# Two half tiles of their own buffers for the high and low parts of every weight tile

## The chip, the cores and the metric

The kernel runs on one core of one Trainium2 chip. The metric is the device time of one execution in microseconds (us). The core has five engines that each work through their own queue of instructions in order: TensorE (PE in the rows; its weight loads have a row of their own, PEld), VectorE (DVE), ScalarE (ACT), GpSimd (POOL) and SyncE (SP), whose queue issues nearly all transfers here. They wait for each other through semaphores.

## The reference, cut to what matters

Two layers over 1024 latent tokens and 256 context tokens, all in float32. Nearly all the work is products with weights:

```python
for layer in range(2):
    u  = modulate(rmsnorm(x,  n1), sh1,  sc1)  @ w_in      # x: 1024 x 1024, w_in: 1024 x 3088
    uc = modulate(rmsnorm(xc, n1), csh1, csc1) @ w_in      # xc: 256 x 1024
    y  = concat(mlstm(u, uc), neighbourhood_attention(u, uc), rglru(u, uc)) @ w_out
    x  = x + g1 * y
    h  = modulate(rmsnorm(x, n2), sh2, sc2)
    x  = x + g2 * (square(relu(h @ w1)) @ w2)              # w1: 1024 x 4096, w2: 4096 x 1024
```

The same is done for the context, except for its output side in the last layer. The twelve modulation vectors of a layer are products of a conditioning vector with `w_mod` (1024 x 6144). The mixers hold small products, scans and a softmax; they are not touched here.

## The kernel before

**Weights.** A weight tile is 128 partitions by 1024 float32 numbers (in two places by 1088): 8 K tiles of 128 columns (`w_fm`, line 204, for products with 128 output columns), or 4 K tiles of 256 or 272 columns. `load_w` (line 185) loads it with one transfer (two for half of the output projection) into `wr`, which has two buffers, and splits it into two float32r parts: ScalarE copies the high part into `wh` (line 200), VectorE subtracts it from the raw tile into the low part `wl` (line 201). `wh` and `wl` have two buffers each. There are 340 such tiles. With `early` (the first of the two tiles of a token-major projection, 16 tiles in all) the split is done in two steps of half the columns into the same buffer. A buffer is free again when the last product that reads any of it is done.

**Products.** The activations are kept as high and low parts too, and each product is three products: high by high, low by high, high by low. `proj_fm` (line 427, products on line 436) makes a 128-column tile of a projection for blocks of 256 or 512 tokens, 24 products for each block, over the K tiles in order. `proj_tm` (line 441, products on line 451) goes over the ten tiles of 128 tokens with two weight tiles, K tiles 0 to 3 in the first and 4 to 7 in the second. `oproj` (products on line 1325) is the output projection in halves of four K tiles.

**The order of the stages**, twice: the LRU's and the mLSTM's input projections beside their scans; the attention's input projections in two groups (`na_group`), the first beside the mLSTM's chunks; the attention with half of the output projection between its steps (from 510 us in layer 0, from 2100 us in layer 1); the other half; then the MLP. `mlp_group` takes 512 hidden columns at a time: four tiles of the first weight (line 436) and four of the second, each of four K tiles (line 1477), whose products VectorE adds to the residual (line 1481). The MLP runs its eight groups first for one part of the tokens and then for the other: in layer 0 for context and first half (256 + 512 columns), then for the second half (512); in layer 1 for 512 and 512. So 24 of its 32 group runs have products of 512 columns only.

**Modulation steps** run beside all this. In layer 0's mLSTM output and attention projections, 32 steps each load 512 KB of `w_mod` into `mr`, one buffer, and TensorE multiplies it (line 274). In layer 0's first MLP part, 48 steps for layer 1 are done by VectorE, 16 or 8 operations each (lines 310 and 312), and every second or fourth step TensorE transposes the sums (`mod_sum`, line 323): 16 sums in all.

**The order of instructions** is not the order of the text. A scheduler sorts each engine's queue when the program is built, by its own model of when operands are ready, so that another shape or another buffer moves instructions on every engine.

## Time and profile before

| | us |
|---|---|
| three executions | 3126.22, 3126.86, 3132.38 |
| their median | 3126.86 |
| span of the profiled execution, first to last instruction | 3122.6 |
| median less that span | 4.3 |
| TensorE busy in the span | 3016.5 |

The profile is of one execution, and durations below are its own. The span leaves out what lies before the first and after the last instruction; the 4.3 us are taken for that. Busy time of TensorE counts each product from its start to its modelled end, and ends overlap the next start, so a small gap between two products need not show as idle time: the distance of two starts tells it.

### The profile page before, as it was taken

To read this page: it belongs to the slowest core of one execution; us is meant where nothing else is said; L and a number is where in the kernel's file an instruction comes from. 1 tells how busy PE (TensorE), PEld (TensorE's weight loads), DVE (VectorE), ACT (ScalarE), POOL (GpSimd) and SP (SyncE) were. 2 spreads that over 40 slices of the span, in tenths; PEclk is the share of its full clock that TensorE was granted. 3 is DMA by queue.
4 is the path that set the end of the run, shared out by engine and by line. 5 is a ranking of instruction groups with operands and counts; after the bars stand their busy time and mean duration, and the time that the engine had idled before them with its cause. 6 is when DMAs were issued, how large, how long until landed. Compare 5 with 4: busy or idle time off the path is not lost.

```text
span 3122.6 us, 47473 instructions
## 1 busy us (share of the span) xinstructions
PE 3016.5 (97%) x18250; PEld 2553.0 (82%) x18250; DVE 1898.7 (61%) x4318; ACT 1129.1 (36%) x2011; POOL 288.9 (9%) x252
## 2 busy tenths in 40 slices
PE   7999998999899999999999999998899999999999
PEld 6888887878788888887778889997787777887877
DVE  5757654887887666455444584755787444444444
ACT  4632223674422222233222453234564223332222
POOL 0410010122200000010000511002222000000000
PEclk9999999999899999999999999999999999999999
DMA  9624667865233444233333532348753332343333
GB/s 272 223 73 124 174 172 206 234 186 176 67 109 109 123 127 124 79 108 99 92 94 95 176 122 82 101 123 222 223 169 113 95 95 88 99 117 90 93 96 93
DMA packets 531098, 410.73 MB, mean 132 GB/s; under 512 B 27580, under 2 KB 496536, under 8 KB 530872
## 3 DMA queue, kind: packets, MB, share of 16 engines
q1 hardware_dynamic: 519448, 387.41, 42.1%
q0 software_dynamic: 8576, 15.00, 1.5%
q10 hardware_dynamic: 2848, 5.28, 0.6%
q8 instruction: 144, 2.36, 0.3%
q14 instruction: 82, 0.67, 0.1%
HBM read 339.72 MB, written 67.53 MB: 130 GB/s over the span
## 4 chain that ended last, share of the span: by engine, by line
PE 70%; DVE 11%; DMA 10%; issue 2%; ACT 2%; SPq 1%; POOL 0%; ACTq 0%; DVEq 0%; POOLq 0%
PE psa L436 15%; PE psa L1477 14%; PE psq L436 5%; PE psp L436 5%; PE psp L1477 5%; PE psq L1477 5%; PE psp L451 4%; DMA mr<-in_w_mod_dram 4%; PE psq L451 4%; PE psp L1325 2%; DVE ma L312 2%; PE psc L718 2%; DVE wl L201 1%; PE psa L1325 1%; PE psb L688 1%
## 5 line engine op out<-in xcount | busy, mean ns | idle before, releaser
L200 ACT ACTIVATE wh<-wr 128x1024 fp32r<-128x1024 f32 (+3 forms) x356 | 361.6, 1021 | 946.5 <-PE psa L1477 307.3
L201 DVE TENSOR_TENSOR wl<-wr,wh 128x1024 fp32r<-128x1024 f32 (+3 forms) x356 | 425.0, 1198 | 386.4 <-ACT wh L200 380.0
L436 PE MATMUL psa<-xlo,wh 128*128 128x512 f32 (+1 forms) x856 | 319.7, 374 | 2.2 <-DVE xlo L412 2.2
L436 PE MATMUL psa<-xh,wh 128*128 128x512 f32 (+1 forms) x856 | 319.4, 373 | 2.4 <-ACT xh L411 2.3
L436 PE MATMUL psa<-xh,wl 128*128 128x512 f32 (+1 forms) x856 | 319.6, 373 | 1.4 <-DVE wl L201 1.4
L1477 PE MATMUL psa<-hl,wh 128*128 128x512 f32 (+1 forms) x768 | 286.0, 373 | 0.6 <-DVE hl L211 0.6
L1477 PE MATMUL psa<-hh,wh 128*128 128x512 f32 (+1 forms) x768 | 284.2, 375 | 0.3 <-ACT wh L200 0.3
L1477 PE MATMUL psa<-hh,wl 128*128 128x512 f32 (+1 forms) x768 | 277.9, 373 | 0.6 <-DVE wl L201 0.6
L1481 DVE SCALAR_TENSOR_TENSOR res<-psa,modt,res 128x512 f32<-128x512 f32 (+1 forms) x192 | 131.0, 693 | 170.3 <-PE psa L1477 169.9
L436 PEld LDWEIGHTS psa<-xh,wh 128*128 128x128 f32 x856 | 162.1, 190 | 33.4 <-ACT xh L411 3.1
L436 PEld LDWEIGHTS psa<-xlo,wh 128*128 128x128 f32 x856 | 162.1, 189 | 33.1 <-DVE xlo L412 2.6
L436 PEld LDWEIGHTS psa<-xh,wl 128*128 128x128 f32 x856 | 162.1, 189 | 32.3 <-DVE wl L201 2.2
L377 POOL TENSOR_TENSOR acc<-acc,nsq 128x512 f32<-128x512 f32 (+1 forms) x56 | 77.9, 1401 | 1026.9 <-ACT nsq L376 976.5
L1477 PEld LDWEIGHTS psa<-hh,wh 128*128 128x128 f32 x768 | 144.3, 188 | 34.6 <-ACT wh L200 8.6
L451 PE MATMUL psp<-wl,xh 128*128 128x256 f32 (+1 forms) x560 | 164.0, 293 | 4.3 <-DVE wl L201 4.2
L1477 PEld LDWEIGHTS psa<-hh,wl 128*128 128x128 f32 x768 | 144.3, 188 | 28.7 <-DVE wl L201 1.5
L1477 PEld LDWEIGHTS psa<-hl,wh 128*128 128x128 f32 x768 | 144.4, 188 | 27.4 <-DVE hl L211 0.8
L210 ACT ACTIVATE hh<-rl 128x512 fp32r<-128x512 f32 (+1 forms) x160 | 93.5, 589 | 202.1 <-DVE rl L1453 202.0
L451 PE MATMUL psp<-wh,xh 128*128 128x256 f32 (+1 forms) x560 | 161.9, 289 | 2.4 <-ACT wh L200 2.4
L451 PE MATMUL psq<-wh,xh 128*128 128x256 f32 (+1 forms) x560 | 161.7, 289 | 1.4 <-ACT usq L605 0.9
L451 PE MATMUL psq<-wl,xh 128*128 128x256 f32 (+1 forms) x560 | 160.6, 287 | 0.0
L451 PE MATMUL psp<-wh,xlo 128*128 128x256 f32 (+1 forms) x560 | 159.9, 286 | 0.0
(409 smaller groups left out, 7328.5 us busy)
## 6 DMA issues: line engine op xcount, KB each, us to landing
wr<-in_w_mlp_dram SPq DMA_DIRECT2D x256, 512.0 KB
mr<-in_w_mod_dram SPq DMA_DIRECT2D x92, 512.0 KB
wr<-in_w_in_dram SPq DMA_DIRECT2D x48, 512.0 KB
tab<-T_d SPq DMA_DIRECT2D x48, 384.0 KB
T_d<-E_d POOLq DMA_DIRECT2D x48, 256.0 KB, 6.6
ab<-row_d SPq DMA_DIRECT2D x36, 256.0 KB
xT_d<-res SPq DMA_DIRECT2D x4, 2048.0 KB
wr<-in_w_out_dram SPq DMA_DIRECT2D x32, 256.0 KB
```

The source lines that it names most:

```text
L200: act.activation(hi[:, a:b], raw[:, a:b], AF.Copy)
L201: dve.tensor_sub(lo[:, a:b], raw[:, a:b], hi[:, a:b].bitcast(F32))
L210: act.activation(hi, src32, AF.Copy)
L312: dve.scalar_tensor_tensor(a, raw[:, k], s[:, k], a, op0=OP.mult, op1=OP.add)
L377: pool.tensor_add(acc[bi], acc[bi], sq[:, :n])
L436: m = pe.matmul(t[:, :n], w[a][:, k, :], X[bi][b][:, k, :], start=(i == 0), stop=(i == 23))
L451: pe.matmul(t[:, :cols], X[bi][b][:, half * 4 + k, o:o + P], ws[half][a][:, k, :], start=(i == 0), stop=(i == 23))
L688: pe.transpose(t[:w, j * P:(j + 1) * P], S[e][:, o:o + w], permT)
L718: pe.matmul(to[64 * e:64 * e + 64, :P], vals[i][:w, 64 * e:64 * e + 64], PT[:w, e, i], start=(i == 0), stop=(i == nt - 1))
L1325: pe.matmul(t[:, :n], w[a][:, k, cc * P:(cc + 1) * P], Y[bi][b][:, k], start=(i == 0), stop=(i == 11))
L1477: m = pe.matmul(t[:, :n], w[a][:, k, cc * P:(cc + 1) * P], H[bi, k][b], start=(i == 0), stop=(i == 3 * GH - 1))
L1481: dve.scalar_tensor_tensor(xr[bi][:, ct], t[:, :n], G2[:, ct, v:v + 1], xr[bi][:, ct], op0=OP.mult, op1=OP.add)
```

## The change

Each half of the columns of a weight tile's high and low part becomes a tile of its own, with its own buffer: `wh` and `wl` have four buffers of 544 columns in place of two of 1088, the same space. Every tile is now split in two steps, first half first, the 16 `early` ones as well, so that ScalarE and VectorE have 680 splits each where they had 356, 324 more. A class `Halves` picks the half by the K tile, so products read what they read before. A half's buffer is free when the last product that reads that half is done. `wr` and its transfers are the same. The rest of the diff takes comments away.

```diff
-    def load_w(src, shape, early=False):
+    WHALF = WSZ // 2
+
+    class Halves:
+        def __init__(self, views, per):
+            self.views, self.per = views, per
+
+        def __getitem__(self, at):
+            p_, k, c_ = at
+            return self.views[k // self.per][p_, k % self.per, c_]
+
+    def load_w(src, shape):
         raw = wp.tile([P, WSZ], F32, name=nm("wr"), tag="wr", bufs=2)
-        hi = wp.tile([P, WSZ], F32R, name=nm("wh"), tag="wh", bufs=2)
-        lo = wp.tile([P, WSZ], F32R, name=nm("wl"), tag="wl", bufs=2)
...
-        cuts = [0, n // 2, n] if early else [0, n]
-        for a, b in zip(cuts, cuts[1:]):
-            act.activation(hi[:, a:b], raw[:, a:b], AF.Copy)
-            dve.tensor_sub(lo[:, a:b], raw[:, a:b], hi[:, a:b].bitcast(F32))
-        return (hi[:, :n].rearrange("p (k c) -> p k c", k=shape[0]),
-                lo[:, :n].rearrange("p (k c) -> p k c", k=shape[0]))
+        per = shape[0] // 2
+        h = n // 2
+        his, los = [], []
+        for i in range(2):
+            hi = wp.tile([P, WHALF], F32R, name=nm("wh"), tag="wh", bufs=4)
+            lo = wp.tile([P, WHALF], F32R, name=nm("wl"), tag="wl", bufs=4)
+            act.activation(hi[:, :h], raw[:, i * h:(i + 1) * h], AF.Copy)
+            dve.tensor_sub(lo[:, :h], raw[:, i * h:(i + 1) * h], hi[:, :h].bitcast(F32))
+            his.append(hi[:, :h].rearrange("p (k c) -> p k c", k=per))
+            los.append(lo[:, :h].rearrange("p (k c) -> p k c", k=per))
+        return Halves(his, per), Halves(los, per)
...
-                         .rearrange("(k p) c -> p k c", p=P), (4, 256), h_ == 0) for h_ in range(2)]
+                         .rearrange("(k p) c -> p k c", p=P), (4, 256)) for h_ in range(2)]
```

TensorE, SyncE and GpSimd have the same instructions as before. Some 2500 of TensorE's 16,800 stand elsewhere in its queue, and 233 of SyncE's 1284. Line numbers after the change are 15 higher (10 higher for the weights' transfer, 14 for the splits). Three places follow; numbers behind names count tiles and differ between the two programs.

**TensorE, at the third weight tile of the second product in an MLP group of layer 0's second part.** `wh_15960` and `wl_15961` are the parts of that tile, `wh_15994` of the fourth; `psa`, `psp`, `psq` are accumulators, one for each block of output columns. Before:

```order
L1477 MATMUL psa_15945<-hh_15887,wl_15927 128x512
L1477 MATMUL psa_15965<-hh_15773,wh_15960 128x512
L1477 MATMUL psa_15965<-hl_15774,wh_15960 128x512
L1477 MATMUL psa_15979<-hh_15773,wh_15960 128x512
L1477 MATMUL psa_15979<-hl_15774,wh_15960 128x512
L1477 MATMUL psp_15999<-hh_15773,wh_15994 128x512
L1477 MATMUL psp_15999<-hl_15774,wh_15994 128x512
L1477 MATMUL psq_16013<-hh_15773,wh_15994 128x512
L1477 MATMUL psq_16013<-hl_15774,wh_15994 128x512
L1477 MATMUL psa_15965<-hh_15773,wl_15961 128x512
L1477 MATMUL psa_15965<-hh_15811,wh_15960 128x512
```

Now, with `wh_16489` and `wl_16490` the first halves of the third tile:

```order
L1492 MATMUL psa_16473<-hh_16407,wl_16456 128x512
L1492 MATMUL psa_16497<-hh_16281,wh_16489 128x512
L1492 MATMUL psa_16497<-hl_16282,wh_16489 128x512
L1492 MATMUL psa_16497<-hh_16281,wl_16490 128x512
L1492 MATMUL psa_16497<-hh_16323,wh_16489 128x512
L1492 MATMUL psa_16497<-hl_16324,wh_16489 128x512
L1492 MATMUL psa_16497<-hh_16323,wl_16490 128x512
L1492 MATMUL psa_16511<-hh_16281,wh_16489 128x512
L1492 MATMUL psa_16511<-hl_16282,wh_16489 128x512
L1492 MATMUL psa_16511<-hh_16281,wl_16490 128x512
L1492 MATMUL psa_16511<-hh_16323,wh_16489 128x512
```

Before, the high parts are multiplied into four accumulators first, and the first product with a low part stands ninth; now it stands third.

**VectorE, the same place.** The first row is the end of the group's first half; the residual sums (`res`) follow, one for each accumulator, and between them the low parts of the third and fourth tile. Before:

```order
L211 TENSOR_TENSOR hl_15888<-rl_15884,hh_15887 128x512
L1481 SCALAR_TENSOR_TENSOR res_9072<-psa_15897,modt_119,res_9072 128x512
L1481 SCALAR_TENSOR_TENSOR res_9072<-psp_15911,modt_119,res_9072 128x512
L1481 SCALAR_TENSOR_TENSOR res_9072<-psq_15931,modt_119,res_9072 128x512
L201 TENSOR_TENSOR wl_15961<-wr_15959,wh_15960 128x1024
L1481 SCALAR_TENSOR_TENSOR res_9072<-psa_15945,modt_119,res_9072 128x512
L201 TENSOR_TENSOR wl_15995<-wr_15993,wh_15994 128x1024
```

Now, with `wl_16490` and `wl_16494` the halves of the third tile, `wl_16528` and `wl_16532` those of the fourth:

```order
L226 TENSOR_TENSOR hl_16408<-rl_16404,hh_16407 128x512
L215 TENSOR_TENSOR wl_16490<-wr_16487,wh_16489 128x512
L1496 SCALAR_TENSOR_TENSOR res_9192<-psa_16421,modt_119,res_9192 128x512
L1496 SCALAR_TENSOR_TENSOR res_9192<-psp_16435,modt_119,res_9192 128x512
L1496 SCALAR_TENSOR_TENSOR res_9192<-psq_16459,modt_119,res_9192 128x512
L215 TENSOR_TENSOR wl_16494<-wr_16487,wh_16493 128x512
L215 TENSOR_TENSOR wl_16528<-wr_16525,wh_16527 128x512
L1496 SCALAR_TENSOR_TENSOR res_9192<-psa_16473,modt_119,res_9192 128x512
L215 TENSOR_TENSOR wl_16532<-wr_16525,wh_16531 128x512
```

The first half of the third tile's low part stands ahead of the three residual sums that it stood behind as a whole.

**SyncE, at the end of layer 0's attention projections (475 to 483 us before).** `mr_3622`, now `mr_3674`, is the weight tile of one modulation step; `wr` are weights of the output projection, `KH` copies of the attention's keys. Before:

```order
L266 DMA mr_3611<-in_w_mod_dram 128x8x128
L642 DMA ut_5784<-u_nq_78 128x2x128
L602 DMA u_nq_78<-uev_5408 128x256
L642 DMA ut_5797<-u_nq_78 128x4x128
L197 DMA wr_5969<-in_w_out_dram 128x2x256 x2
L672 DMA KH_5742<-KH_5742 64x1280
L197 DMA wr_6543<-in_w_out_dram 128x2x256 x2
L266 DMA mr_3622<-in_w_mod_dram 128x8x128
```

Now:

```order
L281 DMA mr_3663<-in_w_mod_dram 128x8x128
L617 DMA u_nq_78<-uev_5397 128x256
L617 DMA u_nq_78<-uev_5428 128x256
L281 DMA mr_3674<-in_w_mod_dram 128x8x128
L617 DMA u_nq_78<-uev_5459 128x256
L207 DMA wr_6057<-in_w_out_dram 128x2x256
L617 DMA u_nq_78<-uev_5490 128x256
L657 DMA ut_5872<-u_nq_78 128x2x128
L281 DMA mr_3812<-in_w_mod_dram 128x8x128
L657 DMA ut_5885<-u_nq_78 128x4x128
L687 DMA KH_5830<-KH_5830 64x1280
L207 DMA wr_6057<-in_w_out_dram 128x2x256
```

The step's transfer stood behind four pieces of `w_out` of 256 KB and a copy of keys; now it stands ahead of them, and the next step's (`mr_3812`) behind one piece.

## Rows read from the trace of the kernel before

**Rows 1.** The page: the span, and TensorE's busy time, share and instructions.
```profile
span 3122.6 us, 47473 instructions
...
PE 3016.5 (97%) x18250; PEld 2553.0 (82%) x18250; DVE 1898.7 (61%) x4318; ACT 1129.1 (36%) x2011; POOL 288.9 (9%) x252
```

**Rows 2.** Stretches: length; PE, PEld, DVE, ACT, POOL busy; PE clock, DMA share, GB/s.
```profile
100.00:510.00 410.00, 391.31 (x3227) 355.47 (x3226) 244.81 (x684) 133.09 (x251) 42.71 (x44) 0.99 0.52 152
510.00:800.00 290.00, 269.72 (x2059) 228.40 (x2058) 224.39 (x669) 166.07 (x406) 68.53 (x41) 0.97 0.67 194
800.00:1120.00 320.00, 310.31 (x1750) 267.29 (x1749) 243.99 (x600) 87.10 (x136) 5.71 (x4) 0.98 0.36 106
1120.00:1840.00 720.00, 719.45 (x3569) 596.05 (x3568) 401.64 (x657) 235.65 (x329) 61.04 (x79) 1.00 0.37 112
1840.00:2140.00 300.00, 285.48 (x2190) 269.68 (x2189) 182.14 (x546) 93.25 (x190) 24.42 (x15) 0.99 0.36 108
2140.00:2400.00 260.00, 241.87 (x1740) 196.62 (x1738) 198.33 (x566) 146.77 (x342) 69.28 (x39) 0.97 0.66 187
```

**Rows 3.** TensorE's waits: waiter, releaser: us in total, times, longest.
```profile
PE psp L451 <- DVE wl L201: 4.2, 3, 2.9
...
PE psp L451 <- ACT wh L200: 2.4, 2, 1.7
...
PE psa L1477 <- ACT wh L200: 0.3, 1, 0.3
```

**Rows 4.** The same view of TensorE's weight loads, line 1477.
```profile
PEld psa L1477 <- ACT wh L200: 8.6, 25, 0.7
...
PEld psq L1477 <- ACT wh L200: 3.0, 10, 0.4
...
PEld psp L1477 <- ACT wh L200: 2.2, 7, 0.4
```

**Rows 5.** Timeline at 1540 us, TensorE: start, duration, in brackets the idle time before.
```profile
1540.36 0.19 PEld L1477 LDWEIGHTS psa<-hh,wh 128*128 128x128 f32 x1 [0.24 <-ACT wh L200]
1540.39 0.47 PE L1477 MATMUL psa<-hh,wh 128*128 128x512 f32 x1
...
1541.53 0.19 PEld L1477 LDWEIGHTS psp<-hh,wh 128*128 128x128 f32 x1 [0.40 <-ACT wh L200]
...
1542.10 0.39 PE L1477 MATMUL psq<-hh,wh 128*128 128x512 f32 x1
```

**Rows 6.** The chain that ended last, a quiet piece: start, duration, instructions.
```profile
1518.20 11.20 PE psa L436 x48
```

**Rows 7.** Instructions by shape, ScalarE: count, busy us, mean ns, idle before.
```profile
L200 ACT ACTIVATE wh<-wr 128x1024 fp32r<-128x1024 f32 x322 | 340.9, 1060 | 910.3 <-PE psa L1477 307.3 <-PE psa L436 197.0 <-PE psq L1477 117.2
...
L200 ACT ACTIVATE wh<-wr 128x512 fp32r<-128x512 f32 x28 | 16.1, 623 | 21.9 <-PE psq L451 13.3 <-PE psb L436 4.3 <-PE psp L436 4.3
```

**Rows 8.** The same view of VectorE.
```profile
L201 DVE TENSOR_TENSOR wl<-wr,wh 128x1024 fp32r<-128x1024 f32 x322 | 398.9, 1240 | 365.0 <-ACT wh L200 358.7
...
L211 DVE TENSOR_TENSOR hl<-rl,hh 128x512 fp32r<-128x512 f32 x128 | 88.4, 690 | 62.2 <-ACT hh L210 61.9
...
L201 DVE TENSOR_TENSOR wl<-wr,wh 128x512 fp32r<-128x512 f32 x28 | 20.8, 772 | 8.9 <-ACT wh L200 8.8
```

**Rows 9.** Timeline of VectorE at 1865 us, layer 1's value projection.
```profile
1865.44 0.69 DVE L1041 TENSOR_TENSOR rshf<-rshf,rope 128x512 f32<-128x512 f32 x1 [0.48 <-DMA rope<-in_k_rope_dram]
1866.05 2.28 DVE L201 TENSOR_TENSOR wl<-wr,wh 128x1024 fp32r<-128x1024 f32 x1
```

**Rows 10.** Timeline of TensorE at 493 us, a modulation step of layer 0.
```profile
493.42 1.08 PE L274 MATMUL psc<-mr,cact 128*32 128x128 f32 x16 [4.96 <-DMA mr<-in_w_mod_dram]
```

**Rows 11.** The chain that ended last: that step's weights on their way.
```profile
482.28 11.10 DMA mr<-in_w_mod_dram
```

**Rows 12.** Waits over the whole kernel: TensorE for modulation products, VectorE for high parts.
```profile
DVE wl L201 <- ACT wh L200: 380.0, 138, 22.3
PE psc L323 <- DVE ma L312: 3.5, 5, 1.1
```

More of the change, by code (lines that the diff above doesn't have):

```diff
@@ L1006, in backbone_kernel @@
                 w2 = [load_w(win[l, h_ * 512:(h_ + 1) * 512, C_MO:C_MO + 272].rearrange("(k p) c -> p k c", p=P),
-                             (4, 272), h_ == 0) for h_ in range(2)]
+                             (4, 272)) for h_ in range(2)]
                 def ev_og(t, tt):
@@ L1048, in backbone_kernel @@
                 w2v = [load_w(win[l, h_ * 512:(h_ + 1) * 512, C_MV:C_MV + 256].rearrange("(k p) c -> p k c", p=P),
-                              (4, 256), h_ == 0) for h_ in range(2)]
+                              (4, 256)) for h_ in range(2)]
                 def ev_v(t, tt):
```

## The prediction

> **What bounds the kernel now.** I read the page first: TensorE is busy 3016.5 of 3122.6 us [rows 1]. Only about 106 us are left in which it visibly stands, and no change that leaves its instructions as they are can win much more. The stretches say where those 106 us lie [rows 2]: the MLP from 1120 to 1840 us has 719.45 of 720 busy, while the projections from 100 to 510 us leave 18.7 us, the attention of layer 0 (510 to 800) 20.3, the first MLP part of layer 0 (800 to 1120) 9.7, and the projections and the attention of layer 1 14.5 and 18.1. Then the view of TensorE's waits, by what ended them. The split weights end ten of its groups: the two largest are 4.2 us for low parts and 2.4 us for high parts in the token-major projections, the smallest 0.3 us [rows 3], and the ten together are 13.2 us in 17 waits. The rest of the idle time is ended by transfers, scores, softmax and evictions, which the change doesn't touch.
>
> The page's idle time misses small gaps, since a product's modelled end (0.39 us) lies beyond the next one's start. In a quiet piece of the MLP 48 products start within 11.20 us, 0.233 us each [rows 6]. At 1540 us, where an MLP group goes to the third tile of its second weight, seven starts lie between 1540.39 and 1542.10: six steps take 1.71 us where 1.40 would do, and the weight loads before two of them stood 0.24 and 0.40 us for a high part [rows 5]. That is 0.31 us lost that no idle time shows. Weight loads on line 1477 wait so 25, 10 and 7 times, 42 in all [rows 4]; at two a place, some 21 of the 24 group runs with 512 columns only lose 0.31 us each, 6.5 us.
>
> **Part 1: buffers that come free earlier, and a first half that is ready earlier.** A whole high part takes ScalarE 1060 ns, a half 623 [rows 7]; a whole low part takes VectorE 1240 ns, a half 690 in the nearest undisturbed row of that shape, 772 as the mean of those that are there [rows 8]. So the first product after a late release can start about 0.44 us earlier on the high side, and 0.44 + 0.55 = 1.0 us earlier on the low side; and the first half's buffer is released half a tile's last use earlier, 12 products or up to 2.8 us [rows 6].
>
> Of the 13.2 us the 6.6 in the token-major projections are the stubborn ones. The largest wait, 2.9 us [rows 3], is for a split at 1866.05 us that took 2.28 us and stood behind a rotary operation which itself waited 0.48 us for its table [rows 9]; in the new order its halves still stand behind that operation. There only the shorter first half helps. I keep 4.0 of the 6.6. The other 6.6 us are 12 waits of 0.3 to 1.0 us, and 1.0 us is what the first half saves; I keep 1.0. That takes away 8.2 us. Bounds: nothing, if the splits are late for other reasons, and all 13.2.
>
> **Part 2: the group places in the MLP.** Before, both tiles in use were released together, so ScalarE made two whole high parts in a row and VectorE made the low part after three residual sums; the scheduler had bridged this by taking only high parts into four accumulators first, and TensorE stood for these. Now the first half of the low part stands ahead of the residual sums, and the products take it third. Its buffer was released more than 20 products before, over 4 us [rows 6], so it should be there. The second half's high part can start when the old tile's second half is done, about nine products or 2.1 us before, and needs 0.62 us. I take the whole 6.5 us; bounds 0 and 24 places by 0.31, 7.4 us.
>
> **Part 3: what the 324 more splits cost.** ScalarE pays 2 x 623 - 1060 = 186 ns for each tile, VectorE 2 x 690 - 1240 = 140 up to 2 x 772 - 1240 = 304 ns [rows 7, 8]. In the MLP this has cover: from 1120 to 1840 us ScalarE is busy 236 and VectorE 402 of 720 us [rows 2], and a tile is prepared while the one before is used. The 256 MLP tiles I cost at nothing there; if that cover were gone, they would cost 256 x 0.33 = 84 us. Outside the MLP 68 tiles are split in two that weren't, 68 x 0.49 = 33 us of work at most on engines that TensorE sometimes waits for. It stands 71.6 of 1260 us in those four stretches, 6% [rows 2], so 2 us of it lie on the path, and I add 0.5 for the first MLP part, where VectorE is busy 244 of 320: 2.5 us. Bounds: 0 and 16, half of the 33.
>
> A row weighs in here: VectorE needs 690 ns for 512 numbers and 1240 for 1024 [rows 8], so 140 ns or more are paid per instruction and not per number.
> The Trainium skill ("VectorE: DVE Perf Modes", the section on the TRN2 errata) speaks against the change with it: small tiles pay a fixed cost each, and a large one pays it once; its formula for a float32 sum of two tensors, (N + 151)/0.96 ns, gives 691 and 1224 ns, and the trace agrees. By that rule alone the sum would get 324 x 157 ns = 51 us, an estimate from that page, if VectorE were what TensorE waits for all the time.
> It isn't: VectorE is busy 61% of the span [rows 1].
>
> **Part 4: the order that the scheduler makes.** Of TensorE's queue 2500 products move, mostly inside the attention, by a few places. I cost that at nothing in the middle, with 6 us on either side: a quarter to a third of the 20.3 us that TensorE stands in layer 0's attention. One move can be read. At 493.42 us TensorE waited 4.96 us for a modulation step's weights [rows 10]; they had been on their way for 11.10 us, since 482.28 [rows 11], behind four pieces of `w_out` and a copy of keys in SyncE's queue. Now they stand ahead of these. The step itself also stands 25 products nearer to the one before, though, and the next step's weights stand behind one such piece. I take 3 us off; bounds are 5 off and 3 on.
>
> **Sum.** -8.2 - 6.5 + 2.5 - 3.0 = -15.2 us. The sum is made against the profiled execution, whose span is 3122.6 us; what lies around it stays, and the median of the three executions is 4.3 us above that span. From 3126.9 this gives 3111.7: 3112 us, 0.5% faster. Its own range is 3104 to 3119, with part 1 between 4 and 11 and part 4 taken to either side.
>
> **The rivals.**
>
> *The waits only change their owner.* The releases come earlier, but ScalarE and VectorE take their instructions in order, and the splits stay behind the same rotary operations, evictions and transfers; a removed wait of 0.5 us is followed by the next late thing, the table of the rotary operation or an eviction. For it: the largest wait [rows 9], and that the token-major projections hold half of the 13.2 us. Against it: the 42 waits on line 1477 have nothing else ahead of them [rows 4, 5]. Then only some 6 us go and 2.5 come: 3123.
>
> *Slower: VectorE in layer 0's first MLP part.* There VectorE is busy 244 of 320 us [rows 2], it also makes 48 modulation steps, and the splits' first halves now stand inside a step's products, where the whole split mostly stood behind them. A low part waits for its high part, and that for TensorE's release: 380 us in 138 waits, 2.75 us each [rows 12]. Such a wait now holds up the step's products, and the 16 transposes of the sums stand in TensorE's queue among the MLP's products, so TensorE stops. Before, five of them waited, 3.5 us in all [rows 12]. If ten more sums are late by 2.75 us each, that is +27 against -15: 3139. It decides from six late sums on. Against it: TensorE hardly stands there now, and the schedule leaves many products between two sums.
>
> *More than the sum: the clock.* The granted clock is 0.97 of full in both attention stretches and 1.00 in the MLP [rows 2]. A mean of 0.97 over layer 0's 290 us is what some 17 us at the lower of its two levels (1.2 of 2.4 GHz) give, and costs at most 9 us there. If fewer stops keep the clock up, up to 5 us per attention come on top: 3102.
>
> **How the numbers follow.** Chances: the forecast 0.55, the clock 0.10, waits that change their owner 0.21, slower 0.14, in which I count a bad order of the attention too. About 0.2%, 6 us, is what a measurement of this kernel can tell from no change, so faster means below 3120.6 us and slower above 3133. The forecast and the clock lie below: with 0.01 of the second case 0.66 faster. The rest of that case is the same, 0.20, and 0.14 are slower. The range must hold 8 in 10: from 3101, with the whole of parts 1 and 2 and the move in part 4 gone (-25.6), to 3130, which takes in the waits that change their owner and a little of the bad cases; it leaves out most of the 0.14 and a few hundredths below.
>
> **What would show it.** Right: the weight loads' waits on the line of rows 4 fall from 42 to a few and the starts at that place lie 0.233 us apart; the splits' groups in TensorE's waits fall from 13.2 to about 5 us, with what is left in the token-major projections; the wait at the modulation step of rows 10 is gone or below 2 us; ScalarE and VectorE have some 60 and 45 to 98 us more of work and TensorE the same. Wrong: TensorE's wait for the sums grows by 10 us or more (the slower rival), or the waits outside the splits grow by as much as the splits' waits fell (the first rival), or the attention stretches are longer by more than 6 us.

## The result, and the profile after

The change makes the kernel slower: 3170.4 us where the kernel before took 3127.8 in the same comparison, ratio 1.0133, 95% interval 1.0118 to 1.0148. The forecast was 3112 and the range ended at 3130; the sign was the other one. The profiled execution has a span of 3168.8 us, 46.2 more than before.

The page's busy line after, to be held against [rows 1]:

```profile
PE 3025.4 (95%) x18250; PEld 2574.3 (81%) x18250; DVE 1939.7 (61%) x4642; ACT 1186.0 (37%) x2335; POOL 274.7 (9%) x252
```

TensorE has the same 18250 products and 9 us more of busy time; the other 37 us are idle time. ScalarE works 56.9 us more, near the 60 that were forecast, and VectorE 41.0, a little under the least that was forecast (45). So most of the loss isn't work, it is waiting, and the first question is where. Products can be counted: the start of the product with the same number in TensorE's queue, in two traces, tells how far one kernel has fallen behind at that point. Each column below is the growth of that delay over a stretch, in us, against the profiled execution before (the last product, 3117.5 us before, stands for the end). The second line is the kernel before traced once more on another chip (named again under the three edits together, below): what no change does.

| stretch, us before | to 142 | to 434 | to 803 | to 1056 | to 1376 | to 1793 | to 2375 | to end | sum |
|---|---|---|---|---|---|---|---|---|---|
| what it is | entry | LRU, mLSTM, L0 | attention, L0 | MLP, L0, first | the same, last 320 us | MLP, L0, second part | projections, attention, L1 | MLP, L1 | |
| before, again | 0.0 | +3.7 | +0.9 | +0.1 | -0.1 | 0.0 | +3.0 | -0.1 | +7.4 |
| with the change | +11.8 | +4.4 | +8.9 | +2.6 | **+35.1** | **-4.5** | -3.9 | **-7.9** | +46.6 |

In the kernel before the entry and the MLP repeat to 0.1 us, so what is lost or gained there is the change's. How much the entry loses is not sure to 3 us: two runs below, in which the queues of TensorE, ScalarE, VectorE and SyncE are those of the changed kernel up to 780 us (the first and the fourth line of the last table), lose 9.2 and 8.8 us there. The projections and the attention differ by 1 to 4 us without any change, and what is not above that isn't explained here. The gain that was forecast is there, 12.4 us in the MLP from 1376 us on. It is buried under 35 us in the last 320 us of layer 0's first MLP part and 9 to 12 at the entry.

TensorE's waits after, as in [rows 3] and [rows 12] (waiter, releaser: us in total, times, longest):

```profile
PE psc L338 <- DVE ma L327: 29.9, 26, 2.5
...
PE psp L1340 <- DVE xs L1357: 8.9, 5, 3.6
PE psp L466 <- DVE wl L215: 8.9, 5, 3.1
...
PE psp L451 <- ACT wh L214: 1.5, 1, 1.5
```

The first line is the transposes of the modulation sums: 29.9 us in 26 waits, where [rows 12] has 3.5 in five. One window shows what it does, 1200 to 1300 us (columns as in [rows 2]), after and then before:

```profile
1200.00:1300.00 100.00, 89.49 (x496) 75.13 (x495) 58.90 (x145) 20.38 (x40) 0.00 (x0) 0.98 0.38 108
```

```profile
1200.00:1300.00 100.00, 100.00 (x577) 87.17 (x576) 62.22 (x131) 21.25 (x30) 0.00 (x0) 1.00 0.36 105
```

A saturated TensorE has become one that does 496 products where it did 577. The same view of the whole stretch that lost 35 us, after and then before:

```profile
1083.70:1438.80 355.10, 329.85 (x1826) 281.47 (x1825) 202.40 (x464) 86.51 (x164) 14.01 (x14) 0.98 0.35 102
```

```profile
1056.00:1376.00 320.00, 319.06 (x1825) 277.35 (x1824) 194.52 (x415) 80.36 (x124) 15.48 (x14) 1.00 0.37 110
```

TensorE stands 25.3 us where it stood 0.9, and is busy 10.8 us longer with the same products. Part of that is the clock: before, it was at the upper of its two levels (2.4 GHz) all through; after, it was four times at the lower (1.2 GHz), 14 us in all, each time after TensorE had stood 1.9 to 2.5 us for the sums. That costs some 7 us.

VectorE has less to do than before in the window from 1200 us, 58.9 of 100 us. It isn't overloaded; it waits, too. VectorE's waits between 1060 and 1340 us, after and then before:

```profile
DVE ma L325 <- DMA mr<-in_w_mod_dram: 92.6, 28, 4.7
DVE hl L226 <- ACT hh L225: 10.8, 24, 0.5
```

```profile
DVE wl L201 <- ACT wh L200: 37.4, 16, 4.8
DVE ma L310 <- DMA mr<-in_w_mod_dram: 30.0, 15, 4.2
```

The wait for high parts is gone from this window. In its place each modulation step waits for its own 512 KB. SyncE's transfers in that place say why, after and then before (start, how long the issue took):

```profile
1147.73 0.37 SPq L207 DMA_DIRECT2D wr<-in_w_mlp_dram  x1
1148.86 0.37 SPq L316 DMA_DIRECT2D mr<-in_w_mod_dram  x1
1158.72 0.37 SPq L207 DMA_DIRECT2D wr<-in_w_mlp_dram  x1
1160.23 0.37 SPq L316 DMA_DIRECT2D mr<-in_w_mod_dram  x1
```

```profile
1145.45 0.37 SPq L197 DMA_DIRECT2D wr<-in_w_mlp_dram  x1
1149.57 0.37 SPq L301 DMA_DIRECT2D mr<-in_w_mod_dram  x1
1152.58 0.37 SPq L197 DMA_DIRECT2D wr<-in_w_mlp_dram  x1
1157.32 0.37 SPq L301 DMA_DIRECT2D mr<-in_w_mod_dram  x1
```

Before, a weight tile's transfer leaves 4.1 and 4.7 us ahead of a step's; after, 1.1 and 1.5 us ahead, so it is still under way when the step's is issued. VectorE's timeline of one step tells where that comes from, after and then before (other instructions left out):

```profile
1155.30 0.29 DVE L325 TENSOR_SCALAR ma<-mr,cact 128x128 f32<-128x128 f32 x1 [4.09 <-DMA mr<-in_w_mod_dram]
1155.51 0.68 DVE L215 TENSOR_TENSOR wl<-wr,wh 128x512 fp32r<-128x512 f32 x1
1156.11 0.73 DVE L327 SCALAR_TENSOR_TENSOR ma<-mr,cact,ma 128x128 f32<-128x128 f32 x2
...
1158.01 0.68 DVE L215 TENSOR_TENSOR wl<-wr,wh 128x512 fp32r<-128x512 f32 x1
...
1159.47 0.73 DVE L327 SCALAR_TENSOR_TENSOR ma<-mr,cact,ma 128x128 f32<-128x128 f32 x2
```

```profile
1151.32 1.23 DVE L201 TENSOR_TENSOR wl<-wr,wh 128x1024 fp32r<-128x1024 f32 x1 [0.16 <-ACT wh L200]
...
1153.38 0.29 DVE L310 TENSOR_SCALAR ma<-mr,cact 128x128 f32<-128x128 f32 x1 [0.43 <-DMA mr<-in_w_mod_dram]
...
1156.56 0.73 DVE L312 SCALAR_TENSOR_TENSOR ma<-mr,cact,ma 128x128 f32<-128x128 f32 x2
```

The whole low part stood ahead of a step's first operation; both halves now stand behind it, and that first operation waits for the step's weights (1148.86 to 1155.30, 6.4 us here). The second half ends at 1158.69; only then is the raw buffer free, and the next weight tile's transfer leaves at 1158.72, just ahead of the next step's, which then lands late in its turn. `mr` has one buffer, so the steps form a closed loop: issue, landing, VectorE's operations, next issue. Its terms, as means over 23 steps before and 27 after between 1060 and 1340 us:

| us | issue to first operation | first to last operation | end to next issue | sum | distance of steps |
|---|---|---|---|---|---|
| before | 3.94 | 4.41 | 0.03 | 8.38 | 8.37 |
| after | 5.08 | 4.62 | 0.04 | 9.74 | 9.77 |

TensorE needs 24 x (0.233 + 0.117) = 8.4 us for a weight tile with 512 and 256 columns, and there is one step a tile. Before, a turn of the loop and a tile took the same time, and TensorE hardly stood. The terms add up to the distance by their making, so this doesn't tell which of the two set the pace; the shortest turns of the loop took 7.7 us, so it had some 0.7 us of slack. After, the turn is 1.4 us longer than the tile, and TensorE waits for the loop. 1.40 us more for each of 28 steps are 39 us; 35.1 were lost. 1.14 of the 1.40 are landing, 0.21 the longer step.

### The profile page after: what moved, and what is told of

Its sections match the earlier page's. It is cut to its first block, busy times and chain, and to the rows that moved or that the text cites. A ratio compares the mean times of both kernels' runs of the same rounds, so it can differ in the third digit from the quotient of the medians.

```text
span 3168.8 us, 48550 instructions
## 1 busy us (share of the span) xinstructions
PE 3025.4 (95%) x18250; PEld 2574.3 (81%) x18250; DVE 1939.7 (61%) x4642; ACT 1186.0 (37%) x2335; POOL 274.7 (9%) x252
## 5 line engine op out<-in xcount | busy, mean ns | idle before, releaser
L214 ACT ACTIVATE wh<-wr 128x512 fp32r<-128x512 f32 (+1 forms) x680 | 424.8, 630 | 905.2 <-PE psa L1492 233.9
L215 DVE TENSOR_TENSOR wl<-wr,wh 128x512 fp32r<-128x512 f32 (+1 forms) x680 | 481.7, 714 | 459.1 <-ACT wh L214 444.1
L1492 PEld LDWEIGHTS psa<-hh,wl 128*128 128x128 f32 x768 | 144.8, 189 | 26.4
L466 PE MATMUL psq<-wh,xlo 128*128 128x256 f32 (+1 forms) x560 | 161.8, 289 | 0.0
```

Of the source, the lines that this page charges most:

```text
L214: act.activation(hi[:, :h], raw[:, i * h:(i + 1) * h], AF.Copy)
L215: dve.tensor_sub(lo[:, :h], raw[:, i * h:(i + 1) * h], hi[:, :h].bitcast(F32))
L466: pe.matmul(t[:, :cols], X[bi][b][:, half * 4 + k, o:o + P], ws[half][a][:, k, :], start=(i == 0), stop=(i == 23))
L1492: m = pe.matmul(t[:, :n], w[a][:, k, cc * P:(cc + 1) * P], H[bi, k][b], start=(i == 0), stop=(i == 3 * GH - 1))
```

## The experiments

The kernel before took 3121 to 3144 us on the later chips, so ratios count; each is to the runs of the kernel before on the same chip. Losses by stretch are in the same columns as above at the end of this section. The recorded texts count the runs as they were planned: the first is half tiles for the step's weights, the second the transfers' order at the entry, the third two steps in the old buffers, the fourth the control of the first, the fifth ScalarE's order at the entry.

**Half tiles for the step's weights.** Opens the loop without touching the splits.

```diff
-        raw = rawpool.tile([P, KT, P], F32, name=nm("mr"), tag="mr", bufs=bufs)
-        d = sp.dma_start(raw, I["w_mod"][l, :, j * P:(j + 1) * P]...)
+        hk = KT // 2
+        raw = []
+        for q in range(2):
+            r_ = rawpool.tile([P, hk, P], F32, name=nm("mr"), tag="mr", bufs=3)
+            d = sp.dma_start(r_, I["w_mod"][l, q * hk * P:(q + 1) * hk * P, j * P:(j + 1) * P]...)
+            raw.append(r_)
```

> The changed kernel, in which a modulation step of layer 0's first MLP part loads its 512 KB of weights into two half tiles, with three half buffers in place of one whole (six times less than two whole would need in space beyond it: 2 KB a partition more). Theory A (the loop of transfers): in the changed kernel the second half of a low part stands in VectorE's queue behind the step's wait for its weights, so the next weight tile's transfer is issued about 1 us ahead of the next step's, both are on their way together, and the step's weights land 5 to 6 us after their issue where they took 3.8; with half a step's weights loaded ahead the loop is open. It expects TensorE's wait for the modulation sums to fall from 29.9 us to 8 or less, VectorE's wait for the step's weights between 1060 and 1340 us from 92.6 to under 40, and the time from 3170 to about 3140 (3132 to 3148). Theory B (VectorE has too much in its queue, with the halves' fixed cost and the transposes placed too early): the waits for the sums stay at 20 us or more and the time at 3158 or more.

Measured: 0.9974 of the kernel before (0.9963 to 0.9986), 3127.8 us, less than the 3132 to 3148 expected. (Two whole tiles would take 4 KB a partition more, so 2 KB is half of that, not a sixth.) TensorE's wait for the sums is gone, and the stretch to 1376 us loses nothing: -1.6 in place of +35.1. VectorE's wait for the step's weights, 1060 to 1340 us:

```profile
DVE ma L332 <- DMA mr<-in_w_mod_dram: 10.7, 7, 2.5
```

Theory B falls: VectorE has the same splits and the same operations in its queue, and TensorE doesn't stand.

**The same for the kernel before**, the control.

> The kernel before with the same three half buffers for a modulation step's weights as in the first experiment, as its control. Before the change TensorE waits 3.5 us in all for the sums, so the loop costs nothing there and the time should stay: 3120 to 3130. If it falls by more than 8 us, the first experiment's gain isn't a repair of what the change did but a gain of its own.

Measured: 0.9957 (0.9940 to 0.9974), 3124.0 us: about 11 us by the medians, beyond the 8 us that were set, so the half tiles have a gain of their own. By the traces 5.2 of it lie in the MLP's first 250 us and 0.9 in the stretch in question; the rest is not placed. So in that stretch the first experiment was a repair: it took away 35.1 + 1.6 us where the control took 0.9. With the loop open, the kernel is no faster with the change (0.9974) than without it (0.9957).

**Only the place of the split.** The kernel before, with whole tiles and whole buffers; VectorE's split is put behind the step's fifth operation.

```diff
-            dve.tensor_sub(lo[:, a:b], raw[:, a:b], hi[:, a:b].bitcast(F32))
+            with (tc.issue_after(mid[-6]) if modq and len(mid) >= 6 else nullcontext()):
+                dve.tensor_sub(lo[:, a:b], raw[:, a:b], hi[:, a:b].bitcast(F32))
...
+                if k == 4 and v == 0:
+                    mid.append(d_.ins)
```

> The kernel before, whole tiles and whole buffers, with one order set by hand in VectorE's queue, in layer 0's first MLP part alone: a low part's split stands behind the first five operations of a modulation step, where it stands ahead of the step before. No halves, no more instructions. Theory A (the place of the split alone makes the loop slow: it stands behind the step's wait for its weights, so the weight tile's transfer is issued late, close ahead of the next step's): the step's weights land 4.8 us or more after their issue (3.9 before, 5.1 with the change), steps follow each other at 9.2 us or more (8.4 and 9.7), TensorE waits 15 us or more for the sums (3.5 and 29.9), and the time is 20 to 40 us longer than the kernel before on this chip: 1.006 to 1.013. Theory B (it needs the halves, by their fixed cost or their number): landing stays at 4.2 us or less, and the time within 8 us of the kernel before.

Measured: 1.0127 (1.0108 to 1.0145), 3174.4 us, nearly the change's own loss without a single half. One step on VectorE, with the first operation of the next, then SyncE's transfers:

```profile
1177.03 0.29 DVE L314 TENSOR_SCALAR ma<-mr,cact 128x128 f32<-128x128 f32 x1 [0.71 <-DMA mr<-in_w_mod_dram]
...
1178.78 1.22 DVE L205 TENSOR_TENSOR wl<-wr,wh 128x1024 fp32r<-128x1024 f32 x1
...
1186.54 0.29 DVE L314 TENSOR_SCALAR ma<-mr,cact 128x128 f32<-128x128 f32 x1 [1.91 <-DMA mr<-in_w_mod_dram]
```

```profile
1180.02 0.37 SPq L200 DMA_DIRECT2D wr<-in_w_mlp_dram  x1
1181.60 0.37 SPq L305 DMA_DIRECT2D mr<-in_w_mod_dram  x1
```

The whole split stands behind the step's fifth operation, and the weight tile's transfer, which waits for it, leaves 1.6 us ahead of the next step's. Over 25 steps: 4.90 us from issue to first operation, 4.96 to the last, 9.88 from step to step; the stretch to 1376 us loses 38.3 us. TensorE's waits from 1040 to 1400 us:

```profile
PE psc L329 <- DVE ma L316: 11.1, 9, 2.7
PE psa L1483 <- DVE wl L205: 9.2, 6, 3.6
PE psq L1483 <- DVE wl L205: 3.7, 1, 3.7
PE psp L1483 <- DVE wl L205: 3.6, 1, 3.6
```

Theory A holds: the place is enough, with what the scheduler moved along with it (304 of VectorE's 4318 instructions and 1178 of TensorE's 18250 stand elsewhere, none of them before 988 us). TensorE's wait for the sums, 15.0 us over the whole kernel, is at the least that was expected, since the waits are shared out otherwise: a whole low part inside the step is late for its own products too, 16.5 us, where the change's first half spares TensorE that.

**The order of the two transfers.** Meant to put a weight tile's transfer behind the step's.

```diff
-            sp.dma_start(raw3[:, i * m:(i + 1) * m], s_)
+            with (tc.issue_after(steps[-9]) if modq and len(steps) >= 9 else nullcontext()):
+                sp.dma_start(raw3[:, i * m:(i + 1) * m], s_)
```

> The changed kernel with one order set by hand in SyncE's queue, in layer 0's first MLP part alone: each weight tile's transfer stands directly behind a modulation step's transfer where it stands directly ahead of it now. All buffers, all splits and VectorE's order of them inside the steps are as in the changed kernel. Between 1060 and 1340 us the step's weights land 5.1 us after their issue in the changed kernel, with the weight tile's transfer 1.2 us ahead of them, and 3.9 us before the change, with that transfer 4 to 8 us ahead; steps follow each other at 9.7 and 8.4 us. Theory A (the two transfers on their way together, with the weight tile's ahead, make the loop slow): landing falls to 4.2 us or less, the distance of steps to 8.9 us or less, TensorE's waits for the sums from 29.9 to under 12 us, and the time to about 3145 (3138 to 3152). Theory B (the second half of a split inside the step is enough to make the loop slow, whatever the order of the transfers): the distance stays at 9.4 us or more, and the time at 3160 or more.

Measured: 1.0112 (1.0088 to 1.0135), landing 4.67 us, distance 9.1, sums' waits 25.7, the stretch at +26.3. Inconclusive: the scheduler moved the splits along by a step, and after the first eight steps the weight tile's transfer was again 0.5 to 2.5 us ahead of the step's. Within this trace the seven steps that had it 3.4 to 8.6 us ahead landed after 3.9 to 4.3 us and followed each other at 8.0 us, the later ones landed after 4.2 to 5.6. Before the change 24 steps with 3.7 to 7.8 us between landed after 3.9 on average, after it 26 with less than 2 us between after 5.1. The packets in the traces say a little more: on average a step's own begin to move 1.2 us after its issue before the change, and after it, with less than 2 us between, 1.8 us. And the longest landings have another thing beside them: in all four over 6 us, of which the step shown above is one, a 16 KB packet of a queue that loads instructions (q8 in the page's list of queues, q14 is another) began to move 2.5 to 3.0 us after the issue. With less than 2 us between, 14 steps without a packet of these two queues landed after 4.8 us and 12 with one after 5.5; before the change it was 3.9 and 4.0. That the two transfers slow each other, and that such packets do, is thus read from traces, not shown by an edit.

**Two steps, old buffers.** The kernel before with `early` for every tile.

```diff
-        cuts = [0, n // 2, n] if early else [0, n]
+        cuts = [0, n // 2, n]
```

> The kernel before, with every weight tile split in two steps into the two whole buffers it has: the change's extra instructions and the earlier first half without the separate buffers. If the gain in the MLP (16 us between 1440 us and the end) comes from the buffers, it is not here: the weight loads of the MLP's second products still wait for high parts, some 30 times or more, and that part of the time is as before. The loss in layer 0's first MLP part by the loop of transfers should be here in part, since 26 of 48 second halves stand inside a step in VectorE's order where 45 do with the change: 10 to 25 us, so 3137 to 3152 in all. If two steps alone cost nothing and only the buffers' release does the harm, it is 3124 to 3132.

Measured: 1.0031 (1.0021 to 1.0042), 3143.2 us, inside the expected band, and the loop agrees with its sum (4.21 + 4.62 + 0.03, distance 8.81; +7.9 us in the stretch). But the MLP isn't as before: it gains 3.2 and 5.0 us of the change's 4.5 and 7.9, and of the 42 waits of its second products' weight loads for high parts one is left, 0.2 us. By these two traces two thirds of the gain in the MLP come from splitting in two, one third from the buffers.

**The entry, two edits.** First the transfers' order: the third weight transfer behind the last input tile's.

```diff
+            with (tc.issue_after(wafter[0]) if len(wafter) > 3 else nullcontext()):
+                sp.dma_start(raw3[:, i * m:(i + 1) * m], s_)
```

> The changed kernel with one order set by hand in SyncE's queue: the third and later weight transfers after the entry stand behind the last input tile's transfer, as they do before the change (in the changed kernel three weight transfers stand ahead of it, before the change two). Theory A: the 12 us that are lost between 60 and 142 us come from that order, 2.8 us of waiting for the input tile at 76 us and the norm and half clock behind it; it expects the input tile to be issued at about 62 us in place of 70.4, no wait of more than 1 us for it, and 3170 to become 3158 (3154 to 3163). Theory B: the halves' extra instructions delay the norm of these tokens on VectorE and ScalarE; it expects the 12 us to stay (3166 to 3173), with TensorE's waits for low parts of the normalized input at 88 to 98 us as they are.

Measured: 1.0125 (1.0105 to 1.0144); the entry still loses 9.0 us, as much as the two runs with the changed kernel's queues there (9.2 and 8.8). The input tile left at 70.0 us, not 62: it stands behind the gates' stores, and those wait for ScalarE. So the edit didn't bring the early transfer that theory A speaks of, and can't judge it. The rival's extra work isn't what the trace shows: the engines stand. ScalarE's timeline of the changed kernel, then TensorE's, then VectorE's:

```profile
58.91 1.15 ACT L214 ACTIVATE wh<-wr 128x512 fp32r<-128x512 f32 x2 [3.18 <-DMA wr<-in_w_in_dram]
59.97 0.71 ACT L426 ACTIVATE xh<-nt,modt 128x512 fp32r<-128x512 f32 x1
```

```profile
59.59 0.38 PE L451 MATMUL psp<-xh,wh 128*128 128x256 f32 x1 [1.52 <-ACT wh L214]
```

```profile
65.04 0.69 DVE L215 TENSOR_TENSOR wl<-wr,wh 128x512 fp32r<-128x512 f32 x1 [3.51 <-ACT wh L214]
65.65 0.68 DVE L516 COPY res<-psa 128x512 f32<-128x512 f32 x1
```

With half buffers free earlier, the scheduler puts two high halves of the third tile ahead of the last normalized K tile. They wait 3.18 us for their transfer. Behind them wait TensorE, the gates, the fourth tile's halves (for the gates' products) and VectorE's copies of the next input tiles: the first of these is at 65.65 us where it was at 60.53. So the second edit sets that order back:

```diff
-            act.activation(hi[:, :h], raw[:, i * h:(i + 1) * h], AF.Copy)
+            with (tc.issue_after(gev1[0]) if gev1 else nullcontext()):
+                act.activation(hi[:, :h], raw[:, i * h:(i + 1) * h], AF.Copy)
```

> The changed kernel with one order set by hand in ScalarE's queue: the high parts of weights that are read after the entry stand behind the first gate activation, as they do before the change; nothing else. In the changed kernel the first two high halves of the third weight tile stand ahead of the last normalized K tile's high part: ScalarE stands there 3.18 us for their transfer, TensorE then 1.52 us for that high part at 59.6 us, the transposes of the last four input tiles begin at 64.9 us in place of 59.9, and their norm is late. Theory A (this place makes the loss at the entry): the transposes begin at 61 us or earlier, and 5 to 10 of the 12 us come back: about 3163 (3159 to 3167). Theory B (the order of transfers and the extra instructions make it, and this wait is covered): the transposes begin earlier but the loss at 142 us stays at 9 us or more: 3167 to 3172.

Measured: the transposes begin at 59.73 us, and the entry's loss is 6.4 us. That is 5.4 less than in the changed kernel's own trace, as theory A said, but only 2.4 to 2.8 less than in the three runs that kept ScalarE's order; so this order makes part of the loss, and how much isn't settled. The time doesn't show it, 1.0144 (1.0122 to 1.0166), slower than expected: layer 1's projections and attention lost 7.9 us in that trace.

**All three edits together, and the kernel before again.**

> The changed kernel with the three edits together: half tiles for a modulation step's weights (first experiment), the input tile's transfer ahead of the third weight transfer (second) and ScalarE's order at the entry (fifth). If the losses add up as the traces show them (35 us in the first MLP part and up to 12 us at the entry), what is left is the gain of the change in the MLP, some 13 to 16 us, less 8 to 10 us in the mLSTM and the attention of layer 0: 0.992 to 0.997 of the kernel before, about 3112 to 3125 against 3130 to 3135. If the entry's loss stays, 0.997 to 1.000.

> The kernel before once more, for its trace on this chip: what two traces of the same kernel differ by at the same place in TensorE's order. Times of the kernel before on the last chip lay at 3127 to 3139 us where they lay at 3126 to 3132 on the first, so stages may differ by some us without any change; a difference of the changed kernel that is smaller than that at its place isn't explained.

Measured: 0.9987 (0.9974 to 1.0001), 3127.7 us, the upper of the two cases though the entry's loss is down to 2.8 us; the two orders together make some 6 us of it or more. With its two accidents mended the change is worth nothing that can be told from zero: it gains 12.5 us in the two later MLP parts and 5.6 with the step's half tiles, and loses 19.4 between 142 and 803 us, of which the kernel before loses 4.6 itself when traced on that chip. The kernel before once more (3131.8 us, one run) is the second line of the first table.

**What is left of it all.** The kernel before with the step's half tiles and with two steps for the MLP's tiles of the last three parts alone.

```diff
-                    proj_fm(w_fm(I["w_mlp1"], l, (g * GH + i) * P), X2, part, ev, banks="pqaaa")
+                    proj_fm(w_fm(I["w_mlp1"], l, (g * GH + i) * P, early=last or part is parts[1]), X2, part, ev, banks="pqaaa")
...
-                    w = w_fm(I["w_mlp2"], l, c2 * 256, r0=g * GH * P, kt=GH, cols=256)
+                    w = w_fm(I["w_mlp2"], l, c2 * 256, r0=g * GH * P, kt=GH, cols=256,
+                             early=last or part is parts[1])
```

> The kernel before with half tiles for a modulation step's weights (as in the fourth experiment, 0.9957 there) and with the split in two steps, into the old whole buffers, for the MLP's tiles from layer 0's second part on and in layer 1 alone. In the third experiment those stretches gained 3.3 and 5.0 us by two steps alone, where the change gained 4.5 and 7.9; elsewhere every tile is split whole, so the losses at the entry, in the attention and in the first MLP part shouldn't come. Expected: 0.993 of the kernel before (0.991 to 0.9955), some 3108 to 3115 us where that takes 3132, faster than both kernels. If two steps in the MLP are worth nothing by themselves, it is 0.9957 again.

Measured: 0.9945 (0.9928 to 0.9962), 3118.9 us: faster than both kernels, a little less than expected. The time alone doesn't tell it from the control's 0.9957; the traces do, by 3.1 and 5.8 us gained in the two later MLP parts, where the control gained nothing (+0.1 and +1.4 us). Its busy line:

```profile
PE 3009.3 (97%) x18250; PEld 2559.5 (82%) x18250; DVE 1905.0 (61%) x4510; ACT 1145.1 (37%) x2203; POOL 287.3 (9%) x252
```

The stretches of the runs, in us as in the first table:

| run | to 142 | to 434 | to 803 | to 1056 | to 1376 | to 1793 | to 2375 | to end |
|---|---|---|---|---|---|---|---|---|
| step's half tiles, with the change | +9.2 | +10.6 | +8.8 | -3.9 | -1.6 | -4.5 | -1.8 | -9.2 |
| the same, kernel before | +0.1 | +3.3 | -1.4 | -5.2 | -0.9 | +0.1 | +4.7 | +1.4 |
| split inside the step, kernel before | -0.1 | +1.8 | +2.1 | +7.0 | +38.3 | 0.0 | +7.0 | 0.0 |
| step's transfer first | +8.8 | +8.3 | +12.6 | +2.5 | +26.3 | -4.5 | -1.6 | -8.0 |
| two steps, old buffers | +5.0 | +4.0 | +7.4 | +2.2 | +7.9 | -3.2 | +2.8 | -5.0 |
| entry: transfers' order | +9.0 | +8.6 | +14.2 | +1.5 | +35.1 | -4.5 | -4.3 | -8.0 |
| entry: ScalarE's order | +6.4 | +4.7 | +10.5 | +0.3 | +32.9 | -4.5 | +7.9 | -7.9 |
| all three | +2.8 | +7.6 | +11.8 | -5.6 | -1.6 | -4.5 | +3.7 | -8.0 |
| step's half tiles, two steps in the later MLP | +0.3 | +3.4 | -5.1 | -3.2 | -0.9 | -3.1 | +8.3 | -5.8 |

## Why the prediction was wrong, point by point

**What bounds the kernel** was right for the MLP and blind for one thing. TensorE's row of 719 busy us in 720 [rows 2] says that nothing waits there; it doesn't say how near the next thing is. The loop of the modulation steps could have been closed from the trace of before: 3.94 us of landing and 4.41 of operations on average, 7.7 us in its shortest turns, against 8.4 for a tile.

**Part 1** (-8.2) failed in size: the splits' waits fell from 13.2 us in 17 to 11.8 in 10. The token-major projections, of whose 6.6 us I kept 4.0, have 8.9 now (line 466, 451 before); the wait of [rows 9] is 3.1 where it was 2.9. There the first rival's reason held, that the splits stay behind the same operations: the halves at that wait still stand behind a rotary operation. The waits didn't change their owner, though; they stayed the splits'.

**Part 2** (-6.5) named the right place and was too small; of its two reasons, the half that is ready earlier did more than the buffers. No weight load of line 1492, 1477 before [rows 4], waits for a split. The view of that line's idle time after:

```profile
its engine sat idle before it (us, times) until:
  DVE res L1496: 2.7, 2
  DVE hl L226: 2.3, 2
  ACT hh L225: 0.6, 2
```

The place of [rows 5], TensorE's timeline after, first and last of 19 products:

```profile
1600.28 0.40 PE L1492 MATMUL psa<-hl,wh 128*128 128x512 f32 x1
...
1604.47 0.40 PE L1492 MATMUL psa<-hh,wl 128*128 128x512 f32 x1
```

18 steps in 4.19 us are 0.233 each, the pace of [rows 6]. The 24 group runs gained 4.5 + 7.9 = 12.4 us, 0.52 each where I had taken 0.31 from one place; where the rest comes from isn't shown. The Trainium skill ("Perfetto Trace Analysis", the section on optimizing Scalar and DVE operations) says that breaking up instructions of an engine that isn't saturated, but makes others wait, may let work be done sooner; here this agrees in the later MLP parts, where two thirds of the gain came from it alone, and not in the first, where the broken-up split was done later.

**Part 3** (+2.5) is the step that failed. Its prices held (after, shapes as in [rows 7, 8]):

```profile
L215 DVE TENSOR_TENSOR wl<-wr,wh 128x512 fp32r<-128x512 f32 x672 | 475.9, 714 | 445.7 <-ACT wh L214 430.7 <-PE psa L451 4.6 <-PE psb L1504 2.8
L214 ACT ACTIVATE wh<-wr 128x512 fp32r<-128x512 f32 x672 | 419.5, 630 | 891.8 <-PE psa L1492 233.9 <-PE psa L451 175.1 <-PE psq L1492 94.8
```

2 x 714 - 1240 = 188 ns and 2 x 630 - 1060 = 200 ns a tile. But I cost the halves by their duration and gave 0.5 us for the first MLP part, since VectorE had time to spare there. What they cost there is their place in VectorE's queue, 35 us. The kernel before with whole splits put at that place has this loss (38.3 us) without any half, so the fixed cost of small instructions, the rule that I had weighed and set aside, isn't what made the kernel slower.

**Part 4** (-3, with 6 either side for the order) was too narrow. The wait of [rows 10] didn't go: two such waits stand at 506.51 and 519.64 us, 1.74 and 3.87 us, and the group fell from 10.8 to 9.6 us. The entry had no term in the sum at all; my stretches began at 100 us, and from 55 us on nothing waits there before (TensorE is busy 86.99 of the 87 us to 142). It lost 9 to 12 us; the two moved halves made part of that, and with the input tile's order most of it. In layer 0's attention the loss, 8.9 us, is beyond my bound. One place is the same in the changed kernel and in the runs on it: VectorE waits for a table of queries, and TensorE for VectorE:

```profile
637.29 0.69 DVE L660 TENSOR_TENSOR ut<-ut,rsn 128x512 f32<-128x512 f32 x1 [4.08 <-DMA ut<-u_nq]
```

```profile
639.61 0.80 PE L1340 MATMUL psp<-yh,wh 128*128 128x256 f32 x2 [3.15 <-DVE xs L1357]
```

Its transfer leaves 2.5 us behind two pieces of a `w_out` tile. That these make it late was not tried; the attention's loss, 7 to 14 us in every run with two steps everywhere, stays open.

**The rivals.** The slower one named the place and the sign; it had 0.14. Its price agrees by luck: it took ten more late sums at 2.75 us, 27 us; 21 more waits of some 1.3 us each were measured, 26.4 us, and the time was 3170 where it said 3139. Its mechanism was wrong in the middle: the low part doesn't hold up the step by waiting for its high part, that wait is gone. The step's wait for its own weights holds up the low part, and that the weight tile's transfer. My argument against it, that the schedule leaves many products between two sums, is no argument in a closed loop: a distance in the queue is used up by a loop that is 1.4 us too slow every time. The clock gave nothing back but took (0.984 in the profiled execution, 0.989 before): some 7 us in that stretch.

## What to carry to other kernels

When an instruction is split or its buffer comes free earlier, price the place where its parts will stand in an in-order queue, and not only their duration: look for the instruction ahead of them that waits for a transfer, and for the buffer that the later part holds until then. Close every single-buffer loop of the trace of before (issue to landing, use, next issue) and compare its shortest turns with the pace of the bound engine; a delay beyond the difference is paid at every turn, however idle the engines in it are. A saturated engine's row tells nothing of how little slack its suppliers have.

## What was not expected of the hardware

A 512 KB transfer took 3.9 us from its issue to the first instruction that used it when the 512 KB ahead of it on the same queue had left 3.7 to 7.8 us before, and 5.1 us on average when they had left less than 2 us before; 4.8 us in the steps in which no instructions were loaded at the same time, 5.5 us in the others. The mean busy share of the transfer engines from 1200 to 1300 us is 0.36 before and 0.38 after (the last column but one of the windows above), so the mean doesn't show it.
